# The second FFN's up product with one Strassen pair in eight instead of two, and the copy of M1 issued behind M1's last product

## The chip, the cores and the metric

The kernel runs on one core of a Trainium2 chip. The metric is the device time of one execution in microseconds (us); the median of several executions is compared. Engines are named as in the profile: PE multiplies (PEld loads its weights), DVE is the vector engine, ACT the scalar engine, POOL is GpSimd, and SP issues the DMAs.

## The reference

Two transformer blocks follow each other on 256 rows of 2048 float32 values. The first has attention, retention, cross-attention and a gated FFN. The second has spatial gating, a linear recurrence and, at its end, this FFN, which is the part that the change touches:

```
h = _rmsnorm(x, norm2_g[l])
up = jnp.einsum('bsd,df->bsf', h, ffn_w_up[l])          # 2048 -> 2 * 6144
up = _causal_dwconv(up, ffn_conv_w[l], ffn_conv_b[l])   # three taps along the rows
gate, val = jnp.split(up, 2, axis=-1)
x = x + jnp.einsum('bsf,fd->bsd', jax.nn.gelu(gate) * val, ffn_w_down[l])
return _rmsnorm(x, final_g)
```

## The kernel before

**Numbers.** Each float32 operand is split into a high part in the format float32r and a low part that is the rest (`split`: ACT casts the high part, line 181, DVE subtracts it, line 182). One product of two operands is three matmuls (`mm3`, lines 199 to 201): high by high, high by low, low by high, each 128x128 by 128x512.

**Weights.** All weights pass through one stream of 1 MB tiles. SP loads a tile into one of three `raw` buffers. `push` takes pieces of it: an ordinary pair of row blocks (kind N) is cut in two pieces of 1024 columns; a Strassen pair (kind S) in four pieces, in the order a, c, b, d. Pieces b and d are sums of weight blocks, which DVE forms first (lines 317, 322 and 323), and c is 512 columns wide. The split pieces lie in rings of five buffers, `wh` for the high and `wl` for the low parts, so the cast of a piece has to wait until PE is through with the piece five places earlier; c lies elsewhere. The program asks for pieces four ahead of their use. A `raw` buffer comes free when the last of its pieces is split.

**The up product.** `quad_group` makes 512 columns of gate and 512 of val for all 256 rows, so the 6144 columns take twelve groups, in three parts of four (`PARTS2`); behind each part stands a piece of the down product. In a group the depth of 2048 is eight pairs of 128-row blocks, and a string names the kind of each: `KINDS` for the first FFN, `KINDS2` for the second. A pair N is eight products (24 matmuls), which go into four accumulators M[2], M[4], M[5] and M[3], in this order. A pair S is seven products (21 matmuls) by Strassen's rule in the Winograd form: M[1] and M[2] from piece a, M[3] from c, M[5] and M[7] from b, M[6] and M[4] from d. M[2] to M[5] lie in four banks called `pg`, and there are only these four: the next group's M[2] takes the bank of this group's M[2]. M[1], M[6] and M[7] lie in four more, `pp`, which the transposes use too.

**The close of a group.** ACT copies M[1] into `m` (line 511). DVE then forms u2 = M[6] + m (512), u3 = M[7] + u2 (513), and at the group's end s[0] = M[2] + m (519), s[1] = M[4] + u3 (522), and the two outputs with M[5] and M[3] (524 to 526). Line 519 is what frees the bank of M[2]. ACT scales the four results by the row norm (1241). A coroutine, `conv_pairs`, works on a group's results while the next group multiplies: transposes on PE (1220), three taps (1205 on ACT, 1208 on DVE), gelu (1225), the product (1226) and the split into operands of the down product. Where the down product has a pair S (places 3 and 5 of eight, in the first two parts only), it also forms sums (132 to 135), which are split in turn.

**Order.** Every engine works its instructions in the order of the program; PE's, DVE's and ACT's lists are laid out by a scheduler of the framework, with its own picture of the times. The first FFN uses the same functions with `KINDS`, eleven groups, and `add_quads` uses the same seven products in the down products.

Of the kernel before, what the change touches and what calls it, by code (L numbers as in the profile page):

```python
# [17 lines left out]
S = 256  # L18
# [5 lines left out]
PARTS = [(0, 4), (4, 8), (8, 11)]  # L24
KINDS = "NSNSNSNN"
PARTS2 = [(0, 4), (4, 8), (8, 12)]
KINDS2 = "NNSNNSNN"
KINDS_DOWN = "NNNSNSNN"
TAIL = 5

# [19 lines left out]
def tile_kernel(ctx, tc, x, xT, mem, memT, par, alibi, rdecay, ident_d, bc_rows, gm_wsT,  # L50
# [3 lines left out]
    V, A, T, G = nc.vector, nc.scalar, nc.tensor, nc.gpsimd  # L54
# [13 lines left out]
    def nm(s):  # L68
        cnt[0] += 1
        return f"{s}_{cnt[0]}"  # L70

    def ft():
        return tpool.tile([P, 2, S], F32, tag="t", name=nm("f"))
# [4 lines left out]
    def flat(f):  # L78
        return f.rearrange("p a b -> p (a b)")
# [72 lines left out]
    def gps():  # L152
        return psg.tile([P, 512], F32, tag="g", name=nm("pg"))

    def sps():
        return pss.tile([P, 512], F32, tag="p", name=nm("pp"))
# [40 lines left out]
    def mm3(out, lh, rh, start, stop):  # L197

        T.matmul(out, lhsT=lh[0], rhs=rh[0], start=start, stop=False)  # L199
        T.matmul(out, lhsT=lh[0], rhs=rh[1], start=False, stop=False)  # L200
        T.matmul(out, lhsT=lh[1], rhs=rh[0], start=False, stop=stop)  # L201
# [71 lines left out]
    def kind(w, u):  # L273
        if w is w_down or w is w_down2:
            return KINDS_DOWN[u % 8] if u < 2 * (PARTS if w is w_down else PARTS2)[-1][0] else "N"
        return KINDS[u] if w is w_gu else KINDS2[u] if w is w_uv else "N"

# [54 lines left out]
    def half(w, g, u, i, n):  # L332
        while pos[1] < len(pieces) and len(feed) < 1 + LOOKAHEAD:
            push()
        w_, g_, u_, i_, hi, lo = feed.pop(0)
        assert w_ is w and (g_, u_, i_) == (g, u, i)
        if isinstance(hi, list):
            return hi, lo
        return [[t[:, k * n:(k + 1) * n] for k in range(t.shape[-1] // n)] for t in (hi, lo)]
# [4 lines left out]
    def tick():  # L344
        for g in list(bg):
            try:
                next(g)
            except StopIteration:
                bg.remove(g)
# [8 lines left out]
    def need(lst, i):  # L358
        while lst[i] is None:
            assert bg  # L360
            tick()
        return lst[i]
# [60 lines left out]
    def gemm_q(wap, g, acts, sums_done):  # L423

        M = [None] * 8
        n = len(acts)
        ks = [kind(wap, u) for u in range(n)]
        total = {m: sum(1 if k == "S" else 2 if m in (2, 3, 4, 5) else 0 for k in ks) for m in range(1, 8)}  # L430
        done = [0] * 8

        def prod(m, a, b):
            if M[m] is None:
                M[m] = gps() if m in (2, 3, 4, 5) else sps()
            done[m] += 1
            mm3(M[m], a, b, done[m] == 1, done[m] == total[m])

        for u in range(n):
            a = need(acts, u)  # L440
            if ks[u] == "N":
                plan = [(0, [(2, 0, 0, 0), (2, 0, 1, 1), (4, 1, 0, 0), (4, 1, 1, 1)]),
                        (1, [(5, 1, 1, 0), (5, 1, 0, 1), (3, "D", 1, 0), (3, "D", 0, 1)])]
                for i, ops in plan:
                    hi, lo = half(wap, g, u, i, 512)
                    for m, t, k, b in ops:
                        prod(m, a.diff(k) if t == "D" else a.blk(k, t), (hi[b], lo[b]))
                    tick()
            else:
                plan = [("a", [(1, a.blk(0, 0), 0), (2, a.blk(1, 0), 1)]),  # L450
                        ("c", [(3, a.sums(3), 0)]),
                        ("b", [(5, a.sums(0), 0), (7, a.sums(2), 1)]),
                        ("d", [(6, a.sums(1), 0), (4, a.blk(1, 1), 1)])]
                for i, ops in plan:
                    hi, lo = half(wap, g, u, i, 512)
                    for m, x, b in ops:
                        prod(m, x, (hi[b], lo[b]))
                    if i in "cd":
                        tick()
                if "S" not in ks[u + 1:]:  # L460
                    sums_done(M)
        return M

    def gemm_sum(wap, g, acts, k0, sums_done):


        M = {}
        n = len(acts)
        ks = [kind(wap, k0 + u) for u in range(n)]
        first, end = ks.index("S") if "S" in ks else n, n - ks[::-1].index("S") if "S" in ks else 0  # L470
        ns, nn = ks.count("S"), ks.count("N")
        total = {11: 2 * nn + ns, 12: 2 * nn + ns, 21: 2 * nn + ns, 22: 2 * nn, 1: ns, 5: ns, 6: ns, 7: ns}
        done = dict.fromkeys(total, 0)

        def prod(m, a, b):
            if m not in M:
                M[m] = gps() if m > 10 else sps()
            done[m] += 1
            mm3(M[m], a, b, done[m] == 1, done[m] == total[m])

        for u in range(n):
            if u == first:
                for v in range(first, end):
                    need(acts, v)
            a = need(acts, u)
            if ks[u] == "N":
                plan = [(0, [(11, a.blk(0, 0), 0), (11, a.blk(1, 0), 1), (21, a.blk(0, 1), 0), (21, a.blk(1, 1), 1)]),
                        (1, [(22, a.blk(1, 1), 0), (22, a.blk(0, 1), 1), (12, a.blk(1, 0), 0), (12, a.blk(0, 0), 1)])]
            else:
                plan = [("a", [(1, a.blk(0, 0), 0), (11, a.blk(1, 0), 1)]),  # L490
                        ("c", [(12, a.sums(3), 0)]),
                        ("b", [(5, a.sums(0), 0), (7, a.sums(2), 1)]),
                        ("d", [(6, a.sums(1), 0), (21, a.blk(1, 1), 1)])]
            for i, ops in plan:
                hi, lo = half(wap, g, k0 + u, i, 512)
                for m, x, b in ops:
                    prod(m, x, (hi[b], lo[b]))
                if not first <= u < end:
                    tick()
            if u == end - 1:  # L500
                sums_done(M)
        return M

    def quad_group(wap, g, acts):

        m, u2, u3 = flat(ft()), flat(ft()), flat(ft())

        def early(M):  # L510
            A.copy(m, M[1])
            V.tensor_tensor(u2, M[6], m, ALU.add)
            V.tensor_tensor(u3, M[7], u2, ALU.add)

        M = gemm_q(wap, g, acts, early)
        s = [flat(ft()), flat(ft())]

        def finish(then):
            V.tensor_tensor(s[0], M[2], m, ALU.add)  # L519
            then(0)  # L520

            behind[0] = V.tensor_tensor(s[1], M[4], u3, ALU.add).ins
            then(1)
            V.tensor_tensor(u2, M[5], u2, ALU.add)
            V.tensor_tensor(u3, M[5], u3, ALU.add)
            V.tensor_tensor(u2, M[3], u2, ALU.add)
            return [u2, u3]

        return s, finish
# [17 lines left out]
    def evac_split(ps, c):  # L547

        res = []
        for t in range(2):  # L550
            hi, lo = flat(rt()), flat(rt())
            split(hi, lo, ps[t], need(c, 0)[:, t:t + 1])
            res.append((hi, lo))
        return res

    def xs(t, g):
        return xt[:, t, 512 * g:512 * g + 512]
# [3 lines left out]
    def add_x(ps, g):  # L561
        for t in range(2):
            V.tensor_tensor(xs(t, g), xs(t, g), ps[t], ALU.add)

    def add_quads(wap, g, acts, k0):

        def early(M):
            m, u2, u3, v = (flat(ft()) for _ in range(4))
            A.copy(m, M[1])
            V.tensor_tensor(u2, M[6], m, ALU.add)  # L570
            V.tensor_tensor(u3, M[7], u2, ALU.add)
            V.tensor_tensor(u2, M[5], u2, ALU.add)
            V.tensor_tensor(v, M[5], u3, ALU.add)
            for x, f in zip(parts, (m, u3, v, u2)):
                V.tensor_tensor(x, x, f, ALU.add)

        parts = [xs(0, 2 * g), xs(1, 2 * g), xs(1, 2 * g + 1), xs(0, 2 * g + 1)]
        M = gemm_sum(wap, g, acts, k0, early)
        for x, i in zip(parts, (11, 21, 22, 12)):
            V.tensor_tensor(x, x, M[i], ALU.add)  # L580
# [191 lines left out]
    for i in range(2):  # L772
# [5 lines left out]
        v = evac_split(gemm_tm(w_in_t, i, h_a), rs1c)  # L778
# [36 lines left out]
    for i in range(2):  # L815
        v = evac_split(gemm_tm(w_in_t, 2 + i, h_a), rs1c)
# [364 lines left out]
    for g in range(2):  # L1181
        ps = gemm_tm(w_in2_t, g, h2_a)
        u = []
# [10 lines left out]
    for g in range(4):  # L1194
        add_x(gemm_tm(w_out2, g, y_a), g)
        spawn(next_in(g, h3_a, sq3, cols("norm2_g_2", 0, 16), None, KINDS2), 1)

# [177 lines left out]
```

## Time and profile before

| | us |
|---|---|
| median of three runs | 2591.85 (2591.35 to 2593.89) |
| the profiled execution | 2591.56 |
| its span, first to last instruction | 2589.8 |
| PE busy in the span | 2548.3 |
| DVE busy | 1964.9 |
| ACT busy | 1447.5 |
| mean granted TensorE clock | 0.994 |

The profiled execution is 1.76 us longer than its span and 0.3 us under the median. Within the span the first FFN's up and down products lie at about 757 to 1394 us and the second FFN's at about 1742 us to the end. A row of a list of instructions reads: start, duration, engine, line, operation, tiles written and read, and in brackets the idle time of the engine before it with what ended it. PE's matmuls overlap, and a row's duration (0.39 us for one 512 columns wide) is longer than the distance to the next start; what a matmul costs is that distance. A row of a table of stretches reads: the stretch, its length, busy time and count of PE, PEld, DVE, ACT and POOL, the granted clock, the DMA engines' share and GB/s.

### The profile page before, as it was taken

Reading aid. Unit: us, or ns where it says so; the run is one execution under the profiler, and the core shown is the slowest. Engines: PE = TensorE matmul, PEld = TensorE weight load, DVE = VectorE, ACT = ScalarE, POOL = GpSimd, SP = SyncE. Lnnn points to the kernel's source line nnn. Section 1 sums busy time; section 2 is a strip of 40 time slices with the busy share of each in tenths; the row PEclk is TensorE's granted clock in tenths of the full one; section 3 lists DMA queues with packets and bytes.
Section 4 is the critical chain, followed back from the end, with each engine's and each line's share of the span. In section 5 each row is a group of like instructions: output and inputs, shape, how many; then the busy total and the mean of one; then the engine's idle time right before and its main releaser. Section 6 shows DMA issues by size and latency. Waiting matters only on the chain.

```text
span 2589.8 us, 31366 instructions
## 1 busy us (share of the span) xinstructions
PE 2548.3 (98%) x12125; PEld 2133.3 (82%) x12125; DVE 1964.9 (76%) x2511; ACT 1447.5 (56%) x1939; POOL 27.4 (1%) x34
## 2 busy tenths in 40 slices
PE   8999999999999999999999999999989998999998
PEld 7888888888888888888888888888878887888787
DVE  6666566556569898998888677867889888987885
ACT  6555554454456554555555566655655565645564
POOL 0000010000000000000000000000000000000000
PEclk9999999999999999999999999999999999999999
DMA  6455555554454655555555564555445554455453
GB/s 250 170 179 203 203 204 185 190 184 159 146 185 173 225 182 208 193 215 186 204 195 199 207 220 163 192 182 191 180 157 192 207 185 163 186 202 204 160 212 135
DMA packets 72724, 490.51 MB, mean 189 GB/s; under 512 B 8192, under 2 KB 8320, under 8 KB 14592
## 3 DMA queue, kind: packets, MB, share of 16 engines
q1 hardware_dynamic: 72576, 488.52, 52.3%
q8 instruction: 95, 1.56, 0.2%
q14 instruction: 53, 0.43, 0.0%
HBM read 486.39 MB, written 2.10 MB: 189 GB/s over the span
## 4 chain that ended last, share of the span: by engine, by line
PE 94%; DVE 3%; DMA 1%; ACT 1%; issue 1%; SPq 0%; POOL 0%; ACTq 0%; POOLq 0%; DVEq 0%
PE pg L199 23%; PE pg L200 23%; PE pg L201 23%; PE pg L375 10%; PE pg L379 5%; PE pp L201 3%; PE pp L200 3%; PE pp L199 3%; DVE wl L182 1%; PE pp L192 1%; PE pp L1220 1%; ACT wh L181 1%; DMA w<-in_w_gu_dram 0%; DMA w<-in_w_in_f_dram 0%; DVE r L182 0%
## 5 line engine op out<-in xcount | busy, mean ns | idle before, releaser
L182 DVE TENSOR_TENSOR wl<-w,wh 128x1024 fp32r<-128x1024 f32 x826 | 1005.3, 1222 | 446.0 <-ACT wh L181 441.8
L181 ACT CAST wh<-w 128x1024 fp32r<-128x1024 f32 x826 | 864.9, 1052 | 731.7 <-PE pg L201 508.7
L199 PE MATMUL pg<-wh,r 128*128 128x512 f32 x2627 | 1006.7, 393 | 22.5 <-DVE f L519 22.1
L200 PE MATMUL pg<-wl,r 128*128 128x512 f32 x2627 | 1026.5, 391 | 0.0
L201 PE MATMUL pg<-wh,r 128*128 128x512 f32 x2627 | 1023.4, 391 | 0.0
L199 PEld LDWEIGHTS pg<-wh,r 128*128 128x128 f32 x2627 | 494.8, 188 | 127.2 <-DVE f L519 20.0
L201 PEld LDWEIGHTS pg<-wh,r 128*128 128x128 f32 x2627 | 494.7, 188 | 103.2
L200 PEld LDWEIGHTS pg<-wl,r 128*128 128x128 f32 x2627 | 495.1, 188 | 100.6
L375 PE MATMUL pg<-r,wh 128*128 128x512 f32 x1152 | 312.4, 398 | 9.0 <-ACT wh L181 7.4
L181 ACT CAST wh<-wt 128x1024 fp32r<-128x1024 f32 x146 | 153.7, 1053 | 155.9 <-PE pg L201 100.2
L375 PEld LDWEIGHTS pg<-r,wh 128*128 128x128 f32 x1152 | 202.5, 190 | 41.0 <-ACT wh L181 7.4
L182 DVE TENSOR_TENSOR wl<-wt,wh 128x1024 fp32r<-128x1024 f32 x146 | 178.2, 1220 | 52.0 <-ACT wh L181 49.8
L379 PEld LDWEIGHTS pg<-r,wl 128*128 128x128 f32 x1152 | 169.1, 191 | 18.3 <-ACT r L184 0.2
L379 PE MATMUL pg<-r,wl 128*128 128x256 f32 x1152 | 177.1, 284 | 0.0
L317 DVE TENSOR_TENSOR wt<-w 128x1024 f32<-128x1024 f32 x73 | 88.9, 1218 | 13.8 <-DMA w<-in_w_uv_dram 5.1
L1208 DVE SCALAR_TENSOR_TENSOR f<-pp,pr,f 128x255 f32<-128x255 f32 (+1 forms) x192 | 90.6, 477 | 8.0 <-ACT f L1205 6.6
L201 PE MATMUL pp<-wh,r 128*128 128x512 f32 x247 | 96.5, 391 | 0.0
L200 PE MATMUL pp<-wl,r 128*128 128x512 f32 x247 | 96.2, 389 | 0.0
L199 PE MATMUL pp<-wh,r 128*128 128x512 f32 x247 | 95.7, 393 | 0.0
L181 ACT CAST r<-f 128x512 fp32r<-128x512 f32 (+1 forms) x100 | 59.2, 592 | 24.6 <-DVE f L536 9.4
L181 ACT CAST r<-w 128x512 fp32r<-128x512 f32 x83 | 50.5, 616 | 38.3 <-DMA w<-in_w_gu_dram 22.4
L182 DVE TENSOR_TENSOR r<-f,r 128x512 fp32r<-128x512 f32 (+1 forms) x100 | 65.1, 651 | 5.3 <-ACT r L181 4.7
(202 smaller groups left out, 1691.3 us busy)
## 6 DMA issues: line engine op xcount, KB each, us to landing
w<-in_w_uv_dram SPq DMA_DIRECT2D x96, 1024.0 KB, 4.8
w<-in_w_gu_dram SPq DMA_DIRECT2D x88, 1024.0 KB, 4.8
w<-in_w_down_dram SPq DMA_DIRECT2D x84, 1024.0 KB, 4.8
w<-in_w_in_t_dram SPq DMA_DIRECT2D x40, 1024.0 KB, 4.8
w<-in_w_in_f_dram SPq DMA_DIRECT2D x39, 1024.0 KB, 4.8
w<-in_w_o_dram SPq DMA_DIRECT2D x16, 1024.0 KB, 4.7
w<-in_w_xk_dram SPq DMA_DIRECT2D x16, 1024.0 KB, 4.8
w<-in_w_xv_dram SPq DMA_DIRECT2D x16, 1024.0 KB, 4.8
```

Of the source, the lines that this page charges most:

```text
L181: A.copy(hi, src)
L182: V.tensor_tensor(lo, src, hi.bitcast(F32), ALU.subtract)
L192: T.transpose(pt[:, k, t * P:(t + 1) * P], src[t][:, c + k * P:c + (k + 1) * P], ident)
L199: T.matmul(out, lhsT=lh[0], rhs=rh[0], start=start, stop=False)
L200: T.matmul(out, lhsT=lh[0], rhs=rh[1], start=False, stop=False)
L201: T.matmul(out, lhsT=lh[1], rhs=rh[0], start=False, stop=stop)
L317: V.tensor_tensor(sums["b"], b[:, 3:4, :].to_broadcast([P, 2, 512]), b[:, 0:3:2, :], ALU.subtract)
L375: T.matmul(ps[m], lhsT=hi[k][:, m * P:(m + 1) * P], rhs=ops[k].both(k % 2), start=begin and k == 0, stop=stop, skip_group_check=True)
L379: T.matmul(ps[m][:, S:], lhsT=lo[k][:, m * P:(m + 1) * P], rhs=ops[k].hi(k % 2), start=False, stop=False, skip_group_check=True)
L1208: V.scalar_tensor_tensor(y[:, j, d:], z[:, j, :S - d], col("ffn_conv_w_2", 96 * (2 - d) + c), y[:, j, d:], ALU.mult, ALU.add)
L1220: T.transpose(pt[:, k, t * P:(t + 1) * P], z[t][:, (2 * p + k) * P:(2 * p + k + 1) * P], ident)
```

## The change

`KINDS2` goes from NNSNNSNN to NNNSNNNN: each of the twelve groups has one pair S, at place 3, and seven pairs N. The activations for places 2 and 5 are prepared as for N, the one for place 3 as for S.

The closing function gets a second argument and is called twice in the last pair S: behind piece a, when it issues the copy of M[1], and behind piece d, when it issues the sums, as before. In `quad_group` and `add_quads` the copy so stands in the program right behind M[1]'s last product, no longer behind piece d. `add_quads` takes its four result tiles before the product instead of in the closing function, where there is a pair S.

```diff
-KINDS2 = "NNSNNSNN"
+KINDS2 = "NNNSNNNN"
...
                     for m, x, b in ops:
                         prod(m, x, (hi[b], lo[b]))
+                    if "S" not in ks[u + 1:] and i in "ad":
+                        sums_done(M, i)
                     if i in "cd":
                         tick()
-                if "S" not in ks[u + 1:]:
-                    sums_done(M)
...
                 for m, x, b in ops:
                     prod(m, x, (hi[b], lo[b]))
+                if u == end - 1 and i in ("a", "d"):
+                    sums_done(M, i)
                 if not first <= u < end:
                     tick()
-            if u == end - 1:
-                sums_done(M)
...
-        def early(M):
-            A.copy(m, M[1])
+        def early(M, i):
+            if i == "a":
+                A.copy(m, M[1])
+                return
             V.tensor_tensor(u2, M[6], m, ALU.add)
             V.tensor_tensor(u3, M[7], u2, ALU.add)
...
     def add_quads(wap, g, acts, k0):
 
-        def early(M):
-            m, u2, u3, v = (flat(ft()) for _ in range(4))
-            A.copy(m, M[1])
+        m, u2, u3, v = (flat(ft()) for _ in range(4)) if kind(wap, k0 + 3) == "S" else [None] * 4
+
+        def early(M, i):
+            if i == "a":
+                A.copy(m, M[1])
+                return
```

Up to the preparation of the second FFN's operands the lists of all engines are the same in both programs, instruction for instruction and wait for wait: there the scheduler had put the copy at the same place already. From there on they differ. In the changed program the lines of the close are 512 (the copy), 514, 515, 521, 524, 526, 527 and 528; the taps are 1210 and 1213.

ACT's list at the third group of the first part, before. The names: `wh_15834` to `wh_15868` are pieces of the next group's pairs 0 and 1, `wh_15900` is piece a of its pair 2, and `r<-f` are splits of the down product's operands, the second of them of the sums:

```order
L181 CAST wh_15834<-w_15816 128x1024
L1205 ACTIVATE f_15699<-pp_15694,pr 128x256
L181 CAST r_15706<-w_15674 128x512
L181 CAST wh_15852<-w_15850 128x1024
L1205 ACTIVATE f_15699<-pp_15694,pr 128x256
L181 CAST wh_15868<-w_15850 128x1024
L181 CAST r_15743<-f_15643 128x512
L181 CAST wh_15900<-w_15898 128x1024
L181 CAST r_15752<-f_15747 128x512
L511 COPY f_15510<-pp_15618 128x512
L1241 ACTIVATE f_15884<-f_15884,s_15123 128x512
```

And in the changed program (`wh_15642` and `wh_15654` are pair 4 of the same group, `wh_15675` is the first half of its pair 5):

```order
L181 CAST wh_15624<-wt_15573 128x1024
L1210 ACTIVATE f_15564<-pp_15559,pr 128x256
L181 CAST wh_15642<-w_15640 128x1024
L181 CAST wh_15654<-w_15640 128x1024
L181 CAST r_15608<-f_15514 128x512
L181 CAST wh_15675<-w_15673 128x1024
L1210 ACTIVATE f_15617<-pp_15612,pr 128x256
L512 COPY f_15486<-pp_15646 128x512
L1210 ACTIVATE f_15666<-pp_15661,pr 128x256
```

The copy has moved from behind a piece of the next group's pair 2 to behind a piece of the same group's pair 5. The rows in front of it are alike in the second to fourth group of each part.

DVE's list at the same close, before; `f_15510` is m, and lines 132 to 135 form the sums for the down product:

```order
L182 TENSOR_TENSOR wl_15901<-w_15898,wh_15900 128x1024
L134 TENSOR_TENSOR f_15747<-f_15643,f_15747 128x128
L135 TENSOR_TENSOR f_15747<-f_15643,f_15747 128x128
L182 TENSOR_TENSOR r_15753<-f_15747,r_15752 128x512
L512 TENSOR_TENSOR f_15511<-pp_15667,f_15510 128x512
L513 TENSOR_TENSOR f_15512<-pp_15659,f_15511 128x512
L519 TENSOR_TENSOR f_15884<-pg_15521,f_15510 128x512
L522 TENSOR_TENSOR f_15885<-pg_15528,f_15512 128x512
```

And in the changed program; `wl_15785` and `wl_15801` are the next group's pair 0, `wl_15819` and `wl_15835` its pair 1:

```order
L182 TENSOR_TENSOR wl_15785<-w_15782,wh_15784 128x1024
L182 TENSOR_TENSOR r_15729<-f_15723,r_15728 128x512
L182 TENSOR_TENSOR wl_15801<-w_15782,wh_15800 128x1024
L182 TENSOR_TENSOR wl_15819<-w_15816,wh_15818 128x1024
L521 TENSOR_TENSOR f_15850<-pg_15495,f_15486 128x512
L524 TENSOR_TENSOR f_15851<-pg_15502,f_15488 128x512
L182 TENSOR_TENSOR wl_15835<-w_15816,wh_15834 128x1024
L317 TENSOR_TENSOR wt_15918<-w_15914 128x1024
```

Before, the two sums with M[6] and M[7] stood directly ahead of the one that frees M[2]; now they stand some ten rows earlier, and the row ahead is the split of the next group's pair 1. The four rows from `L521` on are in this order in eleven of the twelve groups; the last has no `L317`.

## The prediction

> **What bounds the kernel now.** First the page's busy times and the shares of its chain of waits by engine:
>
> ```profile
> span 2589.8 us, 31366 instructions
> PE 2548.3 (98%) x12125; PEld 2133.3 (82%) x12125; DVE 1964.9 (76%) x2511; ACT 1447.5 (56%) x1939; POOL 27.4 (1%) x34
> PE 94%; DVE 3%; DMA 1%; ACT 1%; issue 1%; SPq 0%; POOL 0%; ACTq 0%; POOLq 0%; DVEq 0%
> ```
>
> PE bounds it, so three matmuls more cost their full length, and time can be won only where PE stands still: 41.5 us of the span. To place them I read the busy times by stretches, the first FFN and then two parts of the second:
>
> ```profile
> 757.00:1394.00 637.00, 636.62 (x2856) 527.67 (x2855) 560.33 (x671) 357.99 (x409) 1.64 (x1) 1.00 0.54 197
> 1800.00:2100.00 300.00, 291.51 (x1313) 240.22 (x1312) 256.86 (x328) 172.58 (x213) 0.00 (x0) 0.99 0.51 186
> 2100.00:2400.00 300.00, 291.06 (x1303) 239.40 (x1302) 256.60 (x330) 174.77 (x215) 0.00 (x0) 0.99 0.51 186
> ```
>
> In the first FFN PE idles 0.4 us in 637, with three Strassen pairs in a group; in the second some 9 us in each 300. The list of PE's waits from 1740 to 2520 us names one cause, and the same list for the first FFN one short wait (us in total, times, longest):
>
> ```profile
> PE pg L199 <- DVE f L519: 22.1, 8, 7.0
> PE pg L199 <- DVE f L525: 0.4, 1, 0.4
> ```
>
> A group's first matmul waits until line 519 has read the old M[2] and freed its bank. Three of the eight waits are long, at the third group of each part. PE's list shows them, and one of the five short ones:
>
> ```profile
> 1897.51 0.39 PE L201 MATMUL pg<-wh,r 128*128 128x512 f32 x1
> 1904.90 0.79 PE L199 MATMUL pg<-wh,r 128*128 128x512 f32 x1 [7.01 <-DVE f L519]
> ...
> 1950.45 0.39 PE L201 MATMUL pg<-wh,r 128*128 128x512 f32 x1
> 1951.93 0.47 PE L199 MATMUL pg<-wh,r 128*128 128x512 f32 x1 [1.09 <-DVE f L519]
> 1952.24 0.40 PE L200 MATMUL pg<-wl,r 128*128 128x512 f32 x1
> ...
> 2169.02 0.39 PE L201 MATMUL pg<-wh,r 128*128 128x512 f32 x1
> 2176.42 0.80 PE L199 MATMUL pg<-wh,r 128*128 128x512 f32 x1 [7.01 <-DVE f L519]
> ...
> 2441.40 0.39 PE L201 MATMUL pg<-wh,r 128*128 128x512 f32 x1
> 2446.49 0.80 PE L199 MATMUL pg<-wh,r 128*128 128x512 f32 x1 [4.70 <-DVE f L519]
> ```
>
> Why line 519 is late there, ACT's and DVE's lists tell: ACT at the first long wait, then both engines at the third.
>
> ```profile
> 1898.05 1.04 ACT L181 CAST wh<-w 128x1024 fp32r<-128x1024 f32 x1
> 1901.59 0.62 ACT L181 CAST r<-f 128x512 fp32r<-128x512 f32 x1 [2.50 <-DVE f L135]
> 1902.11 0.58 ACT L511 COPY f<-pp 128x512 f32<-128x512 f32 x1
> ...
> 2441.94 1.04 ACT L181 CAST wh<-w 128x1024 fp32r<-128x1024 f32 x1
> 2442.89 0.58 ACT L511 COPY f<-pp 128x512 f32<-128x512 f32 x1
> ...
> 2444.43 0.68 DVE L512 TENSOR_TENSOR f<-pp,f 128x512 f32<-128x512 f32 x1
> 2445.15 0.69 DVE L513 TENSOR_TENSOR f<-pp,f 128x512 f32<-128x512 f32 x1
> 2445.76 0.68 DVE L519 TENSOR_TENSOR f<-pg,f 128x512 f32<-128x512 f32 x1
> ```
>
> The copy stands on ACT behind `wh_15900`, piece a of the next group's pair 2. Five pieces back in its ring is the second half of this group's pair 7, so the cast can't run before the group's last matmul: it starts 0.15 us after that ends (1897.51 + 0.39, and the same at 2441.40). Only then come the copy, lines 512, 513 and 519, and PE: 4.7 us. In the first two parts the cast of the down product's sums stands between too, which waits 2.50 us for line 135: 7.0 us. It is an order of queues, not a lack of speed.
>
> A long wait has a second price. Three stretches right behind the three long waits, with PE's count second and the granted clock third from the end:
>
> ```profile
> 1904.90:1908.40 3.50, 3.50 (x8) 2.79 (x9) 3.50 (x6) 1.91 (x3) 0.00 (x0) 0.51 0.00 0
> 2176.40:2181.40 5.00, 4.98 (x12) 3.92 (x13) 4.78 (x7) 2.67 (x4) 0.00 (x0) 0.50 0.00 0
> 2446.40:2451.10 4.70, 4.61 (x11) 3.69 (x12) 4.67 (x8) 2.67 (x4) 0.00 (x0) 0.51 0.09 35
> ```
>
> The clock is at half for 3.5 to 5 us. Behind the 1.09 us wait it isn't: the matmul after the first starts 0.31 us later, the next ones at the usual distance.
>
> **The change part by part.** The usual distance is read from the first and the last of 46 matmuls of the same stage:
>
> ```profile
> 1759.65 0.39 PE L199 MATMUL pg<-wh,r 128*128 128x512 f32 x1
> ...
> 1769.85 0.39 PE L199 MATMUL pg<-wh,r 128*128 128x512 f32 x1
> ```
>
> 10.20 us over 45 is 0.227 us.
>
> *More matmuls.* A pair N has 24, a pair S 21, and twelve groups lose one S: 36 matmuls, 36 x 0.227 = **+8.2 us**, all on PE with nothing to hide it. The Trainium skill ("TensorE: Matmul & The Clock Gate", section "Back-to-back issue gap") gives about 131 ns per matmul of 512 columns in a stream of weight loads and matmuls; by that figure the term would be an estimated 4.7 us and the time 3.5 us lower, but the rows here show 227 ns, and the measurement decides.
>
> *Less on DVE and ACT.* From the groups of this stage by shape (mean in ns behind the comma):
>
> ```profile
> L182 DVE TENSOR_TENSOR wl<-w,wh 128x1024 fp32r<-128x1024 f32 x233 | 282.3, 1219 | 56.1 <-ACT wh L181 55.6
> L181 ACT CAST wh<-w 128x1024 fp32r<-128x1024 f32 x232 | 241.8, 1052 | 167.4 <-PE pg L201 114.9 <-PE pp L201 19.0 <-DMA w<-in_w_down_dram 11.9
> L317 DVE TENSOR_TENSOR wt<-w 128x1024 f32<-128x1024 f32 x32 | 39.0, 1218 | 5.1 <-DMA w<-in_w_uv_dram 5.1
> L322 DVE TENSOR_TENSOR wt<-wt,w 128x512 f32<-128x512 f32 x32 | 21.8, 682 | 0.0
> L182 DVE TENSOR_TENSOR r<-w,r 128x512 fp32r<-128x512 f32 x32 | 21.9, 684 | 0.1
> L181 ACT CAST r<-w 128x512 fp32r<-128x512 f32 x32 | 19.6, 612 | 6.9 <-DMA w<-in_w_down_dram 6.4 <-DMA w<-in_w_uv_dram 0.5
> L1205 ACT ACTIVATE f<-pp,pr 128x256 f32<-128x256 f32 x88 | 49.3, 560 | 15.0 <-PE pp L1220 9.5 <-DVE f L1208 5.3
> ```
>
> On DVE a pair S takes the sums (1.22 + 2 x 0.68) and the splits of a, b and d (3 x 1.22) and c (0.68), 6.9 us; a pair N 2 x 1.22. That is 4.5 us less per group, 54 in all; on ACT 3 x 1.05 + 0.61 against 2 x 1.05, 1.7 per group. One activation fewer is prepared as S. All this lies beside PE's work, so I book it at nothing; it only makes the close less tight. A `raw` buffer is held over a pair S, which now happens once per group; weights and DMA issues are as many as before.
>
> *The copy.* With the only S at place 3, M[1] is complete after one product, 18 matmuls of pair 3 and 4 x 24 before the group's end: 114 x 0.227 = 26 us. In the changed order the cast ahead of the copy is the first half of pair 5; five pieces back is piece a itself, which PE leaves three matmuls behind M[1]'s. So the copy ends after 0.7 + 1.05 + 0.56 (a tap, line 1205's row) + 0.58, 2.9 us behind M[1], and the sums with M[6] and M[7] run in the middle of the group.
>
> *The close.* What is late next? The row ahead of line 521 (old 519) is the low part of the next group's pair 1, first half. Five pieces back is pair 6's second half, through 24 matmuls, 5.5 us, before the group's end. Cast 1.05, split 1.22 and line 521's 0.68 put its end 2.5 us ahead of PE's need. M[2] itself is complete 18 matmuls (4.1 us) before the end. This rests on the order shown and on PE, ACT and DVE keeping the pace of these rows. So I take all eight waits as gone. They cost, start to start less 0.23 each, the 22.1 us of idle plus 8 x (0.39 - 0.23), 23.4 us; the slow stretches 3.50 - 8 x 0.227, 5.00 - 12 x 0.227 and 4.70 - 11 x 0.227, together 6.2 us. **-29.6 us**.
>
> *The move of the copy in the first FFN and the down products* is worth nothing: the lists are equal there in the first block, and PE's waits on line 519 lie at up products.
>
> Sum, from the profiled execution: 2591.56 - 29.6 + 8.2 = 2570.2. The first FFN's closes leave 0.4 us in eleven groups; I add as much, and the 0.3 us to the median: **2571 us**, 0.8% faster. What I can't see is bounded from the nearest rows. Below, uneven distances at the closes (0.31 for 0.227 is the one shown) could even out with a lighter DVE; at the most 0.4 us for each of twelve, 2566. Above, each close keeps a wait like the row with 1.09, which is 1.25 start to start, 12 x 1.25 = 15 us, 2586. I take the lower part, since the row it is nearest to, the first FFN's, comes from the same functions with a busier DVE (560 of 637 us).
>
> **The rivals.**
>
> *Short waits stay.* If splits run 3.7 us later than above, the 2.5 us are used up and every close waits up to 1.25 us as at 1951.93: up to 2586. For it: five groups have a short wait now. Against it: DVE loses about a tenth of its work (4.5 us per group of some 45; it is busy 257 in 300).
>
> *The long wait moves (slower).* In nine groups M[6] now takes M[1]'s bank, so its first matmul waits for the copy. Between M[1] and it lie 30 matmuls and four transposes, some 7.2 us, the copy needs 2.9. At 1902.11 the copy ran some 20 us behind M[1], whose last product lies 66 matmuls ahead of that group's end. If ACT's queue still slips by 11 us there, the third groups would wait 2.9 + 11 - 7.2 = 6.7 us and drop the clock again: 3 x (6.7 + 2.1) = 26, 2597. It decides from a slip of 4.3 us on. Against it: no cast ahead of the copy waits for a group's end any more.
>
> *The copy isn't the cause.* If DVE's pace sets line 519 and the waits stay, only the matmuls count: 2600. For it: DVE has the sums of line 135 in that place. Against it: the third part has no such sums and still waits 4.70 us.
>
> *Even short waits cool the clock.* Waits of 1 us at all twelve closes with a slow stretch of 2.1 us each would take 25 us back: 2596. The Trainium skill ("TensorE: Matmul & The Clock Gate", section "A second HAM failure mode: psum-queue depth-cycling") says that short idles between groups, from cycling through PSUM banks, make the clock swing. The rows here speak against it: behind 1.09 us the distance is normal at once.
>
> **How the numbers follow.** About 0.2%, 5 us, is what a measurement of this kernel can tell from no change. Waits gone, 2571 (own range 2566 to 2578): 0.75. Short waits stay, 2578 to 2586: 0.13, most of it still faster. Moved wait, 2597: 0.06. Copy not the cause, 2600: 0.04. Cooled clock, 2596: 0.02. Faster 0.75 + 0.11 = 0.86; same 0.02 + 0.02 = 0.04; slower 0.10. The range 2566 to 2586 leaves out the last three and the edges, under 2 in 10.
>
> **What would show it.** Right: PE's waits from 1740 us on list no line 521, or under 1 us in all; 36 matmuls more at 0.227 us; the clock 1.00 throughout the up product; the copy some 3 us behind M[1]'s matmuls; DVE's busy time about 55 us lower. Wrong: waits of PE for the copy, for line 526 or 527, or for a cast at pair 3's piece c (its split ends about 1 us ahead of PE by the same reckoning), each in all twelve groups; or a distance between matmuls over 0.23 us.

## The result and the profile after

The changed kernel takes 2569.62 us (median of three runs, 2568.99 to 2570.92) against 2591.85 us: a ratio of 0.9913, 95% interval 0.9891 to 0.9936. That is 22.2 us less, 1.4 us below the forecast of 2571 us. The profiled execution took 2568.99 us, 2567.2 of them its span. The page's busy times:

```profile
PE 2547.2 (99%) x12161; PEld 2135.6 (83%) x12161; DVE 1914.8 (75%) x2448; ACT 1428.6 (56%) x1915; POOL 27.5 (1%) x34
```

PE has 36 matmuls more and is busy 1.1 us less, mostly because the slow stretches went; with the waits, its idle time fell from 41.5 to 20.0 us. DVE is busy 50.1 us less and ACT 18.9 us less. The busy times by stretches, the first FFN and then the first part of the second (length, PE, PEld, DVE, ACT, POOL, granted clock, DMA share, GB/s):

```profile
757.00:1394.00 637.00, 636.64 (x2856) 527.41 (x2855) 560.24 (x671) 357.43 (x409) 1.64 (x1) 1.00 0.54 197
1800.00:2100.00 300.00, 300.00 (x1362) 248.15 (x1362) 246.13 (x320) 173.72 (x215) 0.00 (x0) 1.00 0.53 191
```

The first FFN is as it was. In the second PE doesn't idle any more, at full clock; the stretch from 2100 to 2400 us reads the same. The list of PE's waits over the whole run has a single row for line 199 left (the line that reads M[2] is now 521, and the last line of the close 528):

```profile
PE pg L199 <- DVE f L527: 0.4, 1, 0.4
```

It lies in the first FFN. Now one close, that of the third group of part 1, in order of time from three engines' lists: PE's last matmul of M[1], ACT's copy, PE's last matmul of M[2], the reader of M[2] on DVE with the row ahead of it, PE's last matmul of the group and the next group's first, and ACT's cast of the first half of the next group's pair 2:

```profile
1871.87 0.39 PE L201 MATMUL pp<-wh,r 128*128 128x512 f32 x1
...
1874.50 0.57 ACT L512 COPY f<-pp 128x512 f32<-128x512 f32 x1
...
1894.10 0.39 PE L201 MATMUL pg<-wh,r 128*128 128x512 f32 x1
...
1894.30 1.23 DVE L182 TENSOR_TENSOR wl<-w,wh 128x1024 fp32r<-128x1024 f32 x1 [1.49 <-ACT wh L181]
1895.44 0.68 DVE L521 TENSOR_TENSOR f<-pg,f 128x512 f32<-128x512 f32 x1
...
1898.18 0.39 PE L201 MATMUL pg<-wh,r 128*128 128x512 f32 x1
1898.41 0.39 PE L199 MATMUL pg<-wh,r 128*128 128x512 f32 x1
1898.65 1.06 ACT L181 CAST wh<-w 128x1024 fp32r<-128x1024 f32 x1 [0.42 <-ACT f L1246]
```

The copy ends 2.8 us behind M[1], 23 us before the close. Line 521 ends at 1896.12, 2.3 us before PE wants the bank at 1898.41, and the next group starts 0.23 us behind the last matmul, like any other matmul. The cast in the last row is the fifth piece of the next group, as `wh_15900` was before, so it too takes the buffer that PE leaves with the group's last matmul. But here it stands behind the copy and behind line 521, and holds up neither.

### The profile page after: what moved, and what is told of

Same layout as the page of the kernel before. It is cut to its first block, busy times and chain, and to the rows that moved or that the text cites. A ratio compares the mean times of both kernels' runs of the same rounds, so it can differ in the third digit from the quotient of the medians.

```text
span 2567.2 us, 31342 instructions
## 1 busy us (share of the span) xinstructions
PE 2547.2 (99%) x12161; PEld 2135.6 (83%) x12161; DVE 1914.8 (75%) x2448; ACT 1428.6 (56%) x1915; POOL 27.5 (1%) x34
## 4 chain that ended last, share of the span: by engine, by line
PE 97%; DVE 1%; DMA 1%; issue 0%; ACT 0%; POOL 0%; SPq 0%; ACTq 0%; POOLq 0%; DVEq 0%
PE pg L199 24%; PE pg L201 24%; PE pg L200 24%; PE pg L375 10%; PE pg L379 5%; PE pp L201 2%; PE pp L200 2%; PE pp L199 2%; PE pp L192 1%; PE pp L1225 1%; DVE wl L182 0%; DMA w<-in_w_gu_dram 0%; ACT wh L181 0%; DMA w<-in_w_in_f_dram 0%; PE pp L1046 0%
## 5 line engine op out<-in xcount | busy, mean ns | idle before, releaser
L182 DVE TENSOR_TENSOR wl<-w,wh 128x1024 fp32r<-128x1024 f32 x838 | 1021.5, 1223 | 492.1 <-ACT wh L181 488.4
L200 PE MATMUL pg<-wl,r 128*128 128x512 f32 x2687 | 1047.9, 390 | 0.0
L201 PE MATMUL pg<-wh,r 128*128 128x512 f32 x2687 | 1044.0, 390 | 0.0
L199 PE MATMUL pg<-wh,r 128*128 128x512 f32 x2687 | 1034.8, 391 | 0.4 <-DVE f L527 0.4
L201 PEld LDWEIGHTS pg<-wh,r 128*128 128x128 f32 x2687 | 504.5, 188 | 105.1
L199 PEld LDWEIGHTS pg<-wh,r 128*128 128x128 f32 x2687 | 504.5, 188 | 103.6 <-DVE f L527 0.8
L181 ACT CAST wh<-wt 128x1024 fp32r<-128x1024 f32 x122 | 128.4, 1052 | 97.0 <-PE pg L201 49.0
L182 DVE TENSOR_TENSOR wl<-wt,wh 128x1024 fp32r<-128x1024 f32 x122 | 148.7, 1220 | 43.5 <-ACT wh L181 42.4
L1213 DVE SCALAR_TENSOR_TENSOR f<-pp,pr,f 128x255 f32<-128x255 f32 x192 | 87.6, 478 | 2.6 <-ACT f L1210 0.6
L201 PE MATMUL pp<-wh,r 128*128 128x512 f32 x211 | 82.2, 390 | 0.0
L317 DVE TENSOR_TENSOR wt<-w 128x1024 f32<-128x1024 f32 x61 | 74.4, 1219 | 10.4 <-DMA w<-in_w_down_dram 6.4
L199 PE MATMUL pp<-wh,r 128*128 128x512 f32 x211 | 82.0, 393 | 0.0
L1210 ACT ACTIVATE f<-pp,pr 128x256 f32<-128x256 f32 x96 | 53.7, 563 | 24.1 <-DVE f L1213 24.1
```

Source lines behind the costliest of these rows:

```text
L181: A.copy(hi, src)
L182: V.tensor_tensor(lo, src, hi.bitcast(F32), ALU.subtract)
L317: V.tensor_tensor(sums["b"], b[:, 3:4, :].to_broadcast([P, 2, 512]), b[:, 0:3:2, :], ALU.subtract)
L1210: A.activation(y[:, j, :], z[:, j, :], AF.Identity, scale=col("ffn_conv_w_2", 192 + c), bias=col("ffn_conv_b_2", c))
L1213: V.scalar_tensor_tensor(y[:, j, d:], z[:, j, :S - d], col("ffn_conv_w_2", 96 * (2 - d) + c), y[:, j, d:], ALU.mult, ALU.add)
```

## The experiments

Three accounts stood against each other. The **queue** account of the prediction: a row on ACT or DVE that waits for the group's last matmul stands ahead of the copy or of the reader of M[2]. The **load** account: two Strassen pairs are too much for DVE and ACT at the close. And within the queue account it was open which half of the change does it, **the copy's new place or the kinds**. Times of before beside them were 2591.5 to 2592.5 us.

### The two halves apart

The copy edit alone is the changed code with the old kinds:

```diff
-KINDS2 = "NNNSNNNN"
+KINDS2 = "NNSNNSNN"
```

> The copy edit alone: the copy of M[1] and the sums are issued behind the pieces a and d, but two pairs in eight stay Strassen (places 2 and 5). Queue theory (mine): in the third group of each part the copy still stands on ACT behind piece a of the next group's pair 2, which waits for the group's last matmul, so PE's eight waits of 22 us in all and the long ones of 7.0, 7.0 and 4.7 us stay: 2591.9 us, 2589 to 2594. Rival, the early copy carries the gain: the waits go and no matmul is added, 2591.9 - 29.6 = 2562 us.

Measured: 2591.73 us, ratio 1.0 (0.999 to 1.0009). PE's waits of this kernel from 1740 us on:

```profile
PE pg L199 <- DVE f L521: 22.1, 8, 7.0
```

The same eight waits to a tenth. Though the program issues the copy earlier, at the third close ACT still runs it behind the cast of piece a, at 1902.00 us (1902.11 in the kernel before). The kinds alone are the old code with the new string:

```diff
-KINDS2 = "NNSNNSNN"
+KINDS2 = "NNNSNNNN"
```

> The other half alone: one Strassen pair in eight, at place 3, with the copy and the sums issued behind the whole pair as before. Queue theory: the copy is one small row later on ACT than in the change, with nothing ahead of it that waits for a group's end; no waits of PE at the closes, 36 matmuls more: 2569.6 us, 2567 to 2572. Rival, the early copy carries the gain: the waits stay and 8.2 us of matmuls come on top, 2600 us.

Measured: 2569.09 us, ratio 0.9913 (0.9898 to 0.9927), no wait of PE at a close. So in this change the kinds carry the whole gain, and the copy edit nothing that can be measured.

### The order of the queues alone, both ways

First the kernel before with its load and its matmuls, but with piece a's cast held behind the copy on ACT, and the down product's last split held behind the copy and the sums and begun four steps of the coroutine later:

```diff
-            split(hi, lo, src)
+            hold = i == "a" and w is w_uv and copied[0] is not None
+            with tc.issue_after(copied[0]) if hold else nullcontext():
+                split(hi, lo, src)
...
-            A.copy(m, M[1])
+            copied[0] = A.copy(m, M[1]).ins
-            V.tensor_tensor(u3, M[7], u2, ALU.add)
+            summed[0] = V.tensor_tensor(u3, M[7], u2, ALU.add).ins
...
+            for _ in range(4 if p and pause == 2 else 0):
+                yield
+            with tc.issue_after(copied[0]), tc.issue_after(summed[0]):
                 if sums and KINDS_DOWN[i + p] == "S":
```

> The kernel before with its two Strassen pairs, its load and its matmuls; only the order of ACT's and DVE's queues changes: the cast of piece a of the next group's pair 2 is queued behind the copy of M[1], and the down product's last split behind the two sums. Queue theory: in part 3 the wait of 4.70 us goes (under 1 us); in parts 1 and 2 the reader of M[2] still stands behind a split of the Quad sums that waits for the group's end, so 7.0 us become some 4 us each; 4.7 + 2.1 + 2 x 3 = 13 us less, 2579 us, 2574 to 2588. Load theory (the busier DVE and ACT with two Strassen pairs make the close late, whatever stands ahead of the copy): waits and time as before, 2590 to 2594.

Measured: 2583.15 us, ratio 0.9966 (0.9953 to 0.9979). PE's waits from 1740 us on (line 529 now is the one that reads M[3], line 522 the reader of M[2]):

```profile
PE pg L199 <- DVE f L529: 11.5, 6, 2.3
PE pg L199 <- ACT r L181: 1.7, 1, 1.7
PE pg L199 <- DVE f L522: 1.4, 1, 1.4
PE pg L200 <- DVE wl L182: 0.3, 1, 0.3
```

The wait of 4.70 us in the third group of part 3 is gone (PE's two waits in that part end at 2392.78 and 2482.68 us, at the second and fourth close), and the 7.0 us are 1.8 and 2.2. The load is the same, so the order alone moves the long waits. But 14.6 us of waits are left, again eight at closes, and mostly on another line: the last row of the close is late now. It isn't a repair, and its time lies near the 2579 us partly by luck: the long waits fell further than expected, to some 2 us and not 4, and the other closes wait up to 2.3 us.

Second the other way: the changed kernel with its light load, but in all twelve groups the copy and the sums put behind the cast of the next group's pair 2, which waits for this group's last matmul:

```diff
-            A.copy(hi, src)
+            cast[0] = A.copy(hi, src).ins
...
-        M = gemm_q(wap, g, acts, early)
+            M = gemm_q(wap, g, acts, lambda M, i: None)
+            push()
+            with tc.issue_after(cast[0]):
+                early(M, "a")
+            early(M, "d")
```

> The changed kernel with its one Strassen pair, its load and its matmuls; in the second FFN's up product alone the copy of M[1] and the two sums are put, in all twelve groups, behind the cast of the next group's pair 2, first half, which waits for the group's last matmul. Queue theory: twelve waits of about 4.3 us on the reader of M[2], each with 2.1 us of slow clock behind it, 79 us: 2648 us, 2630 to 2660. Load theory: the lighter load absorbs it, 2570 to 2575 us.

Measured: 2647.81 us, ratio 1.0216 (1.0199 to 1.0233). The list of waits, then one close (line 513 is the copy, 515 and 516 the sums, 529 the reader of M[2]):

```profile
PE pg L199 <- DVE f L529: 52.9, 12, 4.4
...
1859.87 0.39 PE L201 MATMUL pg<-wh,r 128*128 128x512 f32 x1
...
1860.29 1.04 ACT L181 CAST wh<-w 128x1024 fp32r<-128x1024 f32 x1 [1.66 <-PE pg L201]
1861.24 0.58 ACT L513 COPY f<-pp 128x512 f32<-128x512 f32 x1
...
1862.51 0.68 DVE L515 TENSOR_TENSOR f<-pp,f 128x512 f32<-128x512 f32 x1
1863.23 0.69 DVE L516 TENSOR_TENSOR f<-pp,f 128x512 f32<-128x512 f32 x1
1863.84 0.68 DVE L529 TENSOR_TENSOR f<-pg,f 128x512 f32<-128x512 f32 x1
...
1864.66 0.77 PE L199 MATMUL pg<-wh,r 128*128 128x512 f32 x1 [4.41 <-DVE f L529]
```

This is the old third group again: last matmul, cast, copy, three sums, PE. Twelve such waits cost 78.2 us over the change. Start to start each is 4.57 us more than a distance, 54.9 us. The windows of 5 us behind the twelve waits hold 12 to 15 matmuls where 22 would fit; at 0.227 us each some 1.9 us per close are missing, 22.5 us in all. Little else moved.

### How many pairs, and where

All of these are the changed code with another string.

```diff
-KINDS2 = "NNNSNNNN"
+KINDS2 = "NNNNNSNN"
```

> The changed kernel with its one Strassen pair at place 5 instead of 3: the same work, M[1] complete two pairs later. Queue theory: the casts ahead of the copy take slots that PE leaves before the group's end, so no waits: 2570 us, 2567 to 2574. Rival, the place of the last Strassen pair (5 in the kernel before) makes the close late: three long waits or more, 2590 us and above.

Measured: 2569.18 us, ratio 0.9912 (0.9897 to 0.9927), no waits. With one pair the late place by itself does nothing.

```diff
-KINDS2 = "NNNSNNNN"
+KINDS2 = "NSNSNNNN"
```

> The changed kernel with two Strassen pairs in eight, at places 1 and 3: the matmuls of the kernel before, the last Strassen pair where the change has it. Queue theory: the copy stands behind the first half of pair 5 as in the change, nothing ahead of the reader of M[2] waits for the group's end: no waits and 36 matmuls fewer, 2569.6 - 8.2 = 2561.4 us, 2559 to 2566. Load theory (two Strassen pairs are too many for DVE and ACT at the close): the waits come back, 2580 to 2592 us.

Measured: 2560.87 us, ratio 0.988 (0.9864 to 0.9897), no waits, and better than the change. Its first part by stretches:

```profile
1800.00:2100.00 300.00, 300.00 (x1363) 248.20 (x1362) 267.57 (x345) 182.51 (x226) 0.00 (x0) 1.00 0.54 194
```

DVE is busy 267.57 us in 300, more than the 256.86 of the kernel before, and PE never waits for it. The load account falls for two pairs. Nor do late weights explain the waits: from 1740 to 2492 us ACT and DVE stand idle for tiles of this matrix for 15.6 us in the kernel before and for 17.8 us here.

```diff
-KINDS2 = "NNNSNNNN"
+KINDS2 = "NNSNSNNN"
```

> The changed kernel with two Strassen pairs at places 2 and 4: the copy early on ACT, the same load as with 1 and 3, but piece a of the next group's pair 2 (whose slot PE leaves with the group's last matmul) has its split on DVE ahead of the reader of M[2] in the third groups. Queue theory: waits only there, some 5, 5 and 3.6 us with the slow clock behind: 2561.4 + 14 + 6 = 2581 us, 2575 to 2588. If only the copy's place on ACT counts: no waits, 2561 us. Load theory: as with places 1 and 3, whatever that gives.

Measured: 2597.38 us, ratio 1.0022 (1.0013 to 1.0032): slower than before. The waits are five, 23.2 us, not the three I expected. One of the two I had missed, at a fourth group:

```profile
1939.04 0.58 ACT L512 COPY f<-pp 128x512 f32<-128x512 f32 x1
...
1950.45 1.04 ACT L181 CAST wh<-w 128x1024 fp32r<-128x1024 f32 x1 [0.94 <-PE pg L201]
...
1951.53 1.23 DVE L182 TENSOR_TENSOR wl<-w,wh 128x1024 fp32r<-128x1024 f32 x1 [0.27 <-ACT wh L181]
1952.67 0.68 DVE L515 TENSOR_TENSOR f<-pp,f 128x512 f32<-128x512 f32 x1
1953.27 0.68 DVE L521 TENSOR_TENSOR f<-pg,f 128x512 f32<-128x512 f32 x1
...
1954.10 0.77 PE L199 MATMUL pg<-wh,r 128*128 128x512 f32 x1 [3.73 <-DVE f L521]
```

The copy runs 15 us before PE goes on, and still the close waits: now it is the split on DVE, of a cast released by PE's last matmul, that stands ahead of line 515 and of the reader. An early copy is not enough. The expectation counted such a split in the third groups alone; the two fourth groups, with the slow clock behind them, are most of what it missed.

```diff
-KINDS2 = "NNNSNNNN"
+KINDS2 = "SNSNSNNN"
```

> The changed kernel with three Strassen pairs, at places 0, 2 and 4: 72 matmuls fewer than the change, 16.3 us. By the rows of the groups DVE then needs about 47.5 us per group of 42 us on PE, so I expect DVE to bind: PE waits spread over the group instead of the close, 2565 us or more, up to 2610. Should the load not bind and only the close count: 2553 us, and with waits at the third groups as with places 2 and 4, 2573 us.

Measured: 2647.57 us, ratio 1.0214 (1.0199 to 1.0229), well above the range. At closes PE waits nine times, 65.1 us in all. The wait of 9.50 us that ends at 1970.63, on DVE and ACT:

```profile
1959.54 0.58 ACT L512 COPY f<-pp 128x512 f32<-128x512 f32 x1
...
1967.31 0.62 ACT L181 CAST r<-f 128x512 fp32r<-128x512 f32 x1 [1.69 <-DVE f L135]
...
1968.56 0.68 DVE L514 TENSOR_TENSOR f<-pp,f 128x512 f32<-128x512 f32 x1
...
1969.89 0.68 DVE L521 TENSOR_TENSOR f<-pg,f 128x512 f32<-128x512 f32 x1
```

I expected DVE to be out of time. It isn't at this close: the cast that it needs waits 1.69 us for its own line 135, the last of the down product's sums, and the first sum of the close runs 9 us behind its copy, behind the split of those. By these rows it is order again, though no run changed that order with this load. The copy is late as well: it ends 1 us before the group's last matmul does, and in three other places PE waits for a copy itself, 4.9 us in all. To see load without this, the last pair has to be at 3:

```diff
-KINDS2 = "NNNSNNNN"
+KINDS2 = "NSSSNNNN"
```

> The changed kernel with three Strassen pairs at places 1, 2 and 3: as with places 1 and 3, the last one is at 3, so the copy of M[1] has nothing ahead of it that waits for the group's end; 36 matmuls fewer than with two. Places 0, 2 and 4 could not tell load from order, since their last pair is at 4. If only the order of the queues counts: no waits, 2560.9 - 8.2 = 2552.7 us. Load theory for three: with places 1 and 3 DVE is busy 40.5 us in a group period of 44.1; one Strassen pair more makes it 45.0 in a period of 43.4, so DVE falls 1.6 us a group behind and PE must wait, with slow clock where a wait is long: 2552.7 + 12 x 1.6 = 2572 us without slow clock, 2565 to 2600. I expect the second.

Measured: 2589.78 us, ratio 0.9993 (0.9983 to 1.0002), within the range. PE's waits, two of seven rows, and the first part by stretches:

```profile
PE pg L199 <- DVE f L521: 11.1, 6, 2.9
PE pp L199 <- DVE f L1213: 3.2, 4, 0.8
...
1800.00:2100.00 300.00, 289.84 (x1294) 235.70 (x1293) 274.71 (x355) 179.73 (x225) 0.00 (x0) 0.99 0.50 183
```

No wait is over 2.9 us, and they are spread over all seven rows, the conv's taps among them, with DVE busy 92%. That fits a DVE with no slack, but 8% of its time is still free, so how much is load and how much order stays open.

### Two pairs with the old copy

```diff
-KINDS2 = "NNSNNSNN"
+KINDS2 = "NSNSNNNN"
```

This one is the code of before, with the copy and the sums behind the whole pair.

> Two Strassen pairs at places 1 and 3, but with the copy and the sums issued behind the whole pair, as in the kernel before: the best version without the copy edit. If the places alone carry its time: no waits, 2561 us, 2559 to 2563. If the tighter load with two pairs needs the early copy: short waits at the closes, 2563 to 2576 us.

Measured: 2585.9 us, ratio 0.9982 (0.9973 to 0.9992), 25.0 us above the same kinds with the early copy, and above both times that were expected. DVE's list at the second close, first of this kernel, then of the one with the early copy (lines 519 and 521 read M[2]):

```profile
1851.80 1.23 DVE L182 TENSOR_TENSOR wl<-wt,wh 128x1024 fp32r<-128x1024 f32 x1 [0.90 <-ACT wh L181]
...
1854.75 0.68 DVE L519 TENSOR_TENSOR f<-pg,f 128x512 f32<-128x512 f32 x1
```

```profile
1849.03 0.68 DVE L521 TENSOR_TENSOR f<-pg,f 128x512 f32<-128x512 f32 x1
...
1850.61 1.23 DVE L182 TENSOR_TENSOR wl<-wt,wh 128x1024 fp32r<-128x1024 f32 x1 [0.30 <-ACT wh L181]
```

The copy of this group starts at 1840.71 us in this kernel, at 1828.56 us in the other. The later one is still 12 us ahead of the group's end, so it isn't its own time that PE waits for. What differs at the close is DVE's order: here the reader stands behind the split of a Strassen piece of the next group (`wl<-wt`) and three more rows, with the early copy ahead of that piece. None of these rows waits for the group's last matmul, which starts at 1852.96 us; DVE simply comes to the reader too late, and PE waits 2.23 us. So the copy edit can be worth 25 us, though it is worth nothing with the kinds that it came with. That the order to which it leads the scheduler makes the whole 25 us is read from this close, not shown by a run of its own.

### One place later

What is left to try is the place of the next group's first Strassen pair: at 2, its piece a takes the slot that PE leaves last. So two pairs, the last one at 5 as before, the first at 3:

```diff
-KINDS2 = "NNNSNNNN"
+KINDS2 = "NNNSNSNN"
```

> The changed kernel with two Strassen pairs at places 3 and 5: the load of the kernel before and its last Strassen pair at 5, only the first one a place later. The pieces of the next group's first Strassen pair then come two pieces later in the queues, and nothing ahead of the copy of M[1] or of the reader of M[2] waits for the group's end. Queue theory: no waits, 2561 us, 2559 to 2566. Rival, it is the late last Strassen pair that makes the close late when there are two: waits as before, 2580 to 2592 us.

Measured: 2561.42 us, ratio 0.988 (0.9863 to 0.9896), no waits. And the kernel before with that string and nothing else:

```diff
-KINDS2 = "NNSNNSNN"
+KINDS2 = "NNNSNSNN"
```

> The kernel before with its first Strassen pair at place 3 instead of 2 and nothing else changed: the copy and the sums issued behind the whole pair. The lists show the same rows ahead of the reader of M[2] in all but one or two groups. Queue theory: 2561 us as with the early copy, 2559 to 2566. Rival, the early copy is needed as with places 1 and 3: short waits at the closes, 2575 to 2590 us.

Measured: 2560.6 us, ratio 0.9879 (0.9864 to 0.9893). Its first part by stretches, and the third close on ACT, DVE and PE (511 is the copy, 519 the reader; then PE's last matmul of the group and the next group's first, and the cast that takes the slot left last):

```profile
1800.00:2100.00 300.00, 300.00 (x1363) 248.29 (x1362) 265.76 (x345) 180.57 (x224) 0.00 (x0) 1.00 0.54 193
...
1889.61 0.61 ACT L181 CAST r<-f 128x512 fp32r<-128x512 f32 x1
1890.13 0.58 ACT L511 COPY f<-pp 128x512 f32<-128x512 f32 x1
...
1891.48 0.68 DVE L512 TENSOR_TENSOR f<-pp,f 128x512 f32<-128x512 f32 x1
1892.20 0.69 DVE L513 TENSOR_TENSOR f<-pp,f 128x512 f32<-128x512 f32 x1
1892.81 0.68 DVE L519 TENSOR_TENSOR f<-pg,f 128x512 f32<-128x512 f32 x1
...
1895.88 0.39 PE L201 MATMUL pg<-wh,r 128*128 128x512 f32 x1
1896.10 0.39 PE L199 MATMUL pg<-wh,r 128*128 128x512 f32 x1
...
1896.35 1.06 ACT L181 CAST wh<-w 128x1024 fp32r<-128x1024 f32 x1
```

The copy still stands behind the cast of the down product's sums, 5 us before the close, and the two sums stand directly ahead of the reader, as in the kernel before; all that is missing ahead of them is the row that waits for the last matmul. That row still exists: the first half of pair 2, now of kind N, is cast at 1896.35 us, but behind all of these. So the place of the pair works through the order that the scheduler makes of it; why it puts this cast ahead of the copy when pair 2 is of kind S isn't shown. One letter moved by one place takes 31.9 us from the kernel before, and the Strassen pair that the change gave up costs some 9 us without need.

## Why the prediction was right

*The sum.* Both terms can be read apart. The waits: the kernel before and the one with pairs at 1 and 3 have the same matmuls, and differ by 30.8 us (2591.63 - 2560.87); the string NNNSNSNN alone gives 31.9. The prediction had -29.6. The matmuls: one pair at 5 against two at 1 and 3, both without waits, differ by 8.3 us (2569.18 - 2560.87), 0.23 us each; the prediction had +8.2 at 0.227, and medians that scatter by some 1 us don't tell the two apart. Sum of the measured terms: -22.5, against -22.2 in the times. The 1.4 us by which the forecast was high lie in the first term (30.8 for 29.6) and in the 0.4 us that was added for the second FFN's closes, which have no wait.

The Trainium skill's figure of 131 ns per matmul ("TensorE: Matmul & The Clock Gate", section "Back-to-back issue gap") would have made the term an estimated 4.7 us. The 8.3 us speak against it.

*The diagnosis* was right for the three long waits: a cast that waits for the group's last matmul, ahead of the copy and so ahead of the reader of M[2]. Taking that cast from the copy's way removes the 4.70 us wait with the load unchanged, and putting one there makes twelve. The five short waits, 3.4 us in all, are another matter; the prediction gave no cause for them. DVE's rows ahead of the one of 1.09 us, in the kernel before:

```profile
1949.37 1.21 DVE L182 TENSOR_TENSOR wl<-w,wh 128x1024 fp32r<-128x1024 f32 x1
1950.50 0.68 DVE L513 TENSOR_TENSOR f<-pp,f 128x512 f32<-128x512 f32 x1
1951.10 0.68 DVE L519 TENSOR_TENSOR f<-pg,f 128x512 f32<-128x512 f32 x1
```

Nothing here waits for the last matmul (1950.45 us); DVE works row after row, with a split between the two sums. These waits went too when the pair moved by one place, with the load unchanged.

*The copy* is the step that claimed too much. The prediction lets the close come right because the copy runs 2.9 us behind M[1], in the middle of the group. It does (2.8 us), but that isn't what decides: without the copy edit the time is the same, with it alone nothing changes, with pairs at 2 and 4 an early copy leaves 23.2 us of waits, and with pairs at 3 and 5 a copy late in the group leaves none. What decides the long waits is whether the cast that takes the slot freed last, or its split, stands ahead of the reader of M[2] or behind it. In the change, and in the kernel before with NNNSNSNN, it is the first half of pair 2, of kind N, and stands behind; in the kernel before it is piece a and stands ahead at the third close. The prediction named that piece, but not that moving it is enough.

*The close.* Line 521 was put 2.5 us ahead of PE's need; it ends 2.3 us ahead. M[2] is complete 18 matmuls before the end, as said (1894.10 to 1898.18). With pairs at 1 and 3 the order of rows around this place differs between two kernels that lie 25 us apart.

*Less on DVE and ACT.* DVE's busy time fell by 50.1 us, not by 54: consecutive instructions overlap a little (at 1894.30 one of 1.23 us is followed 1.14 us later), so a sum of means is too much by some 0.1 us for each; for the 60 rows of pair S that went beyond those of pair N these are some 5 us. ACT's fell by 18.9, near 12 x 1.7. As booked, neither bought time: with DVE at 267.57 of 300 PE doesn't wait.

*The rivals.* No short wait stayed and none moved to the copy. "The copy isn't the cause, DVE's pace is" was half right: the copy's new place isn't the cause, but DVE's pace as such isn't either, since the same load runs without a wait in another order. The cooled clock is below.

## What to carry to other kernels

Where a group's first instruction waits for the last reader of the group before, list what stands ahead of that reader on each in-order engine, and look among those rows for one that itself waits for the group's last matmul; moving that row, here by shifting one Strassen pair by one place, took off 31.9 us, while the lighter load that came with the change gained nothing on top and cost 8.3 us of matmuls. An edit that gives up a saving to loosen such a close should first be tried without giving it up. Two edits made together tell what neither is worth: here one carried all of the gain, and the other only showed its worth with a third arrangement.

## What the runs showed of the hardware

The clock falls behind shorter waits than the prediction knew of. Five windows of 5 us right behind a wait, the granted clock third from the end: behind 1.09 us (the copy edit alone), 2.03 us and twice 2.23 us (pairs at 1 and 3 with the old copy), and 4.41 us (the late copy):

```profile
1952.30:1957.30 5.00, 4.95 (x22) 4.13 (x23) 4.83 (x7) 2.06 (x5) 0.00 (x0) 1.00 0.47 192
```

```profile
1901.90:1906.90 5.00, 4.57 (x12) 3.14 (x13) 4.28 (x8) 2.62 (x5) 0.00 (x0) 0.66 0.11 13
2394.80:2399.80 5.00, 5.00 (x24) 4.12 (x25) 4.68 (x7) 3.21 (x5) 0.00 (x0) 1.00 0.61 211
2441.40:2446.40 5.00, 5.00 (x15) 3.98 (x16) 4.52 (x6) 1.95 (x3) 0.00 (x0) 0.66 0.61 213
```

```profile
1812.80:1817.80 5.00, 4.96 (x12) 3.92 (x13) 4.71 (x7) 2.66 (x4) 0.00 (x0) 0.50 0.00 2
```

At 4.41 us the clock is at half for this whole window; behind the other eleven waits of that length the windows read 0.51 to 0.66. At 2.0 to 2.2 us it may fall or not: both waits of 2.03 us cool it (a further wait of some 0.4 us stands at the end of their windows), and of two waits of the same 2.23 us in one run one has 24 matmuls behind it and one 15. At 1.09 us it stays, and so it does behind 1.74 and 1.83 us in the run with the cast behind the copy. Why one of two equal waits cools the clock isn't shown.

The Trainium skill ("TensorE: Matmul & The Clock Gate", section "HAM oscillation — how this bites in real kernels") gives the rule to keep PE's idle gaps under some 3.4 us; here gaps of 2.0 to 2.2 us already cost a slow stretch in part of the cases, so by these runs the bound to keep is under 2 us. The Trainium skill ("TensorE: Matmul & The Clock Gate", section "A second HAM failure mode: psum-queue depth-cycling") lets frequent short idles between groups make the clock swing; behind the single waits of about 1 us no run here shows it.
